# Products of a chunked recurrence on TensorE: both heads as one full-size product, and other regroupings

## The chip, the core and the metric

The kernel runs on one core of a Trainium2 chip. The metric is the device time of one execution in microseconds; lower is better. The engines are TensorE (PE in the profile: matrix products, with PEld for its weight loads), VectorE (DVE), ScalarE (ACT), GpSimd (POOL), and SyncE (SP), from whose queue all transfers are issued. Each engine works through its own queue in the order in which the program was written; semaphores tie the queues together.

## The reference

One step of a two-layer hybrid decoder for a prompt of 512 tokens and 8 sampled sequences of 8 tokens (576 columns in all), model width 1024, inner width 2048, 32 heads of 64. Layer 1 is RWKV-7 time mixing, layer 2 a causal pooling mixer. The part that matters is the recurrence of layer 1, per head a 64 by 64 state S:

```python
def wkv7_scan(S0, r, w, k, v, a, b):
    def step(S, inp):
        r_t, w_t, k_t, v_t, a_t, b_t = inp
        Sa = jnp.einsum('bhij,bhj->bhi', S, a_t)
        S = S * w_t[:, :, None, :] + Sa[..., None] * b_t[:, :, None, :] + v_t[..., None] * k_t[:, :, None, :]
        return S, jnp.einsum('bhij,bhj->bhi', S, r_t)
```

The inputs r, k, v and a gate z are projections of the normed input; the decay w and the rate a come from two low-rank paths. After the scan follow a group norm per head, a bonus term, the gate, and an output projection that is added to the residual stream. Then comes the pooling layer and a last norm.

## The kernel before

The recurrence is computed in chunks of 64 tokens: 8 chunks of the prompt, and the 64 sampled tokens as a ninth. Two heads make a pair (q = 0, 1) that fills the 128 partitions; 16 pairs (m). All products of the recurrence are in fp32, where one product is two instructions of TensorE; the projections are split into high and low parts and run as three reduced-precision products of 128 by 128 by 288 columns ("dense" here).

The work is a graph of operations. `Plan` holds them with nominal costs, and a list scheduler (`order`) writes out one fixed order for all engines from costs, from rotating buffers that must be free, and from a due time for each operation: the table `DUES`, by label (stage letter and number within the stage), plus a step per pair. Labels count on within a stage (`plan.n`), so an operation that disappears shifts the labels behind it unless the counter is moved by hand.

Three stretches follow one another. `front` computes k, v, the decay and what the recurrence needs, and spills it to DRAM (`a_d`, `bk_d`, `bkt_d`, `vt_d`, `p_d`). `rproj` makes r. Then the 16 pairs go through four steps, several pairs at a time:

- `prep(m)`: loads RA (a and r, rows of 576 columns) and BK (L964 to L978), makes the A products (L988: per chunk and head, 64 rows by 128 columns by 128 columns), masks them (L1001 to L1021), and inverts a triangular 32 by 32 block on GpSimd in 31 steps (L1049, L1055), through a round trip over DRAM; two small product groups (L1084, L1098) make the off-diagonal corner. The inverse stands in TI, 64 columns per chunk.
- `recur(m)`: the chain over the chunks. Each hop has three product steps, each one product per head with 64 output rows: the right-hand side (L1158, L1161), the solution with TI (L1180), and the state's change (L1198). Between them stand ScalarE copies out of PSUM (L1174, L1186) and VectorE's update of the state (L1211), which takes the decay at the chunk's end from Pc, loaded from `p_d` (L1116). The sampled sequences have products of their own (L1231, L1257), and the outputs two products per chunk and head (L1280, L1283), written chunk by chunk.
- `after(m)`: group norm, transposes back (L1376), gate, output projection (L1406, dense).
- `zgate(m)`: the gate's projection (L1428, dense).

PSUM in this stage: two banks "pa" for A products, corner, state update and transposes, two "ch" for the chain, one "yy" for outputs, one "sx" for the sampled sequences, two "oo" for the dense products. RA has 4 buffers, SV, UV and BKT 2 each, BK and the inverse's tiles one.

Of the kernel before, what the change touches and what calls it, by code (L numbers as in the profile page):

```python
# [26 lines left out]
# columns of the packed constants  # L27
# [7 lines left out]
# columns of the packed per-channel parameters  # L35
# [44 lines left out]
# where the scheduler's choices lie: a due time per operation of a stage ("-": as the code gives it), and per block a step  # L80
# [91 lines left out]
DXV, MK, ML, MV, MZ, MR = (0, 1), (0, 1, 2, 3), (), (0, 2, 4, 6), (), (0, 2, 4, 6)    # blocks whose mixing DVE does  # L172
NTI, NZ = 3, 2


class Later:
    """a tile that is allocated in the course of the plan"""
# [8 lines left out]
class Plan:  # L186
    """Operations with nominal costs (ns), and a list scheduler that puts them in order.  use: instances of rotating
    buffers, held from the first operation that uses one until the last has ended.  dense: projections, which run beside
    the small products of the recurrence at an even share, so that the tensor engine's clock stays up."""
    ENG = ["PE", "ACT", "DVE", "POOL", "SP", "NIL"]  # L190
    # from the end of one engine's operation to the start of another's that needs it; a transfer's issue
# [13 lines left out]
    def op(self, eng, dur, fn, need=(), use=(), due=0.0, dense=0, work=(0.0, 0.0)):  # L205
        """work: of a product's time the part that depends on the clock, and what it counts for the clock"""
# [8 lines left out]
    def order(self):  # L215
# [19 lines left out]
        taken = {b: [] for b in bufs}            # instances in the order in which they were taken  # L235
        held, done = {}, {}                      # instance: end of its users so far; released at
# [5 lines left out]
        while any(cand.values()):  # L242
            best = None
            for e in self.ENG:
                lo, pick = 1e17, []
                for i in cand[e]:
                    t = max(ready[i], free[e])
                    if ops[i][6] == 1 and share < 0:
                        t = max(t, free[e] - share / RATE)
                    for u in ops[i][4]:  # L250
                        if u not in held:
                            q, n = taken[u[0]], bufs[u[0]]
                            if len(q) >= n:
                                t = max(t, done.get(q[-n], 1e18))
# [59 lines left out]
def body(tc, nc, a):  # L314
# [18 lines left out]
    X1 = kp.tile([128, 16, T], F32R, name="X1")  # L333

# [35 lines left out]
    def split(src, hi, lo, hi_eng=None, lo_eng=None):  # L370
        """src = hi + lo, exact, both in the tensor engine's reduced float32"""
# [16 lines left out]
    def proj(ps, tag, ws, xs, nm, nk=8):  # L388
        """two bank tiles [128, HT] of  W^T x ; ws: list of (hi, lo) units of 8 k blocks"""
# [12 lines left out]
    def rsqrt(y, x, t, mul, eps):  # L402
        """y = (x mul + eps)^-1/2: Newton's iteration from the exponent's half, to float32's accuracy; x, t are used up"""
# [23 lines left out]
    def front(plan, bf, fps, fsb):  # L427
        """norm, token shift, k, v, decay and what goes into the recurrence"""
# [15 lines left out]
        # ---- norm  # L444
# [51 lines left out]
        # ---- mixes; order of mu: r, w, k, v, a, g  # L496
        lseq = []        # the low-rank mixes go in order
# [39 lines left out]
        # low-rank stage 1  # L537
# [21 lines left out]
        def pv(t):      # token columns as (chunk, 64) and (sequence, 8)  # L559
            return (t[:, :TP].rearrange("p (c j) -> p c j", j=64), t[:, TP:].rearrange("p (c j) -> p c j", j=8))  # L560
# [1091 lines left out]
```

## Time and profile before

| | us |
|---|---|
| median of 3 runs | 1626.28 |
| lowest, highest | 1624.1, 1642.92 |
| span of the profiled execution | 1632.8 |

| engine | busy us | share of the span |
|---|---|---|
| TensorE | 1487.4 | 91% |
| VectorE | 1020.8 | 63% |
| GpSimd | 729.6 | 45% |
| ScalarE | 638.4 | 39% |

The profile is of one execution. Its own time is given as the span from the first to the last instruction; what lies around the span isn't known apart from the median of the runs beside it. "Busy" counts instructions as the hardware recorded them. Ends of products are modelled and overlap, so distances between starts tell more of TensorE than durations do. The granted clock is the share of full speed that the throttle let through: 1.00 is 2.4 GHz, 0.50 is 1.2 GHz.

### The profile page before, as it was taken

Reading aid. Unit: us, or ns where it says so; the run is one execution under the profiler, and the core shown is the slowest. Engines: PE = TensorE matmul, PEld = TensorE weight load, DVE = VectorE, ACT = ScalarE, POOL = GpSimd, SP = SyncE. Lnnn points to the kernel's source line nnn. Section 1 sums busy time; section 2 is a strip of 40 time slices with the busy share of each in tenths; the row PEclk is TensorE's granted clock in tenths of the full one; section 3 lists DMA queues with packets and bytes.
Section 4 is the critical chain, followed back from the end, with each engine's and each line's share of the span. In section 5 each row is a group of like instructions: output and inputs, shape, how many; then the busy total and the mean of one; then the engine's idle time right before and its main releaser. Section 6 shows DMA issues by size and latency. Waiting matters only on the chain.

```text
span 1632.8 us, 33010 instructions
## 1 busy us (share of the span) xinstructions
PE 1487.4 (91%) x12544; PEld 1307.6 (80%) x12544; DVE 1020.8 (63%) x2007; ACT 638.4 (39%) x1663; POOL 729.6 (45%) x1374
## 2 busy tenths in 40 slices
PE   5678988987698999999999999999989999999996
PEld 4567888887687877777777777777767999999996
DVE  4688888889456443666666656566567574546223
ACT  3445544454332233444444434444434334234211
POOL 5956665658200533565656555556511240534000
PEclk8689998997898985899999989899899999999998
DMA  3026766564787774555555555554322332222221
GB/s 123 24 68 211 222 203 205 187 200 161 216 281 229 214 260 122 140 161 160 155 158 154 153 147 153 140 134 136 113 65 67 93 104 79 91 96 82 78 78 71
DMA packets 161359, 234.04 MB, mean 143 GB/s; under 512 B 76976, under 2 KB 94704, under 8 KB 161200
## 3 DMA queue, kind: packets, MB, share of 16 engines
q1 hardware_dynamic: 161200, 231.92, 47.2%
q8 instruction: 99, 1.62, 0.4%
q14 instruction: 60, 0.49, 0.1%
HBM read 162.30 MB, written 69.56 MB: 142 GB/s over the span
## 4 chain that ended last, share of the span: by engine, by line
PE 59%; DMA 8%; DVE 6%; issue 2%; SPq 1%; ACT 1%; POOL 1%; DVEq 0%; ACTq 0%; POOLq 0%
PE oo L1406 7%; PE ooz L1428 5%; PE oor L924 4%; PE paA L988 4%; PE ch L1198 2%; DMA SV<-vt_d 2%; PE u L384 2%; PE zz L384 2%; PE u L386 2%; PE u L385 2%; PE zz L386 2%; PE zz L385 2%; PE oo L386 2%; PE oo L384 2%; PE oo L385 2%
## 5 line engine op out<-in xcount | busy, mean ns | idle before, releaser
L1049 POOL TENSOR_TENSOR tm<-X,R 108x84 f32<-108x84 f32 (+23 forms) x465 | 146.7, 316 | 194.9 <-DMA TI<-xd 127.2
L1055 POOL TENSOR_TENSOR X<-X,tm 108x84 f32<-108x84 f32 (+23 forms) x465 | 150.2, 323 | 36.3 <-DMA TI<-xd 0.2
L372 ACT CAST wh_w<-wf_w 128x1024 fp32r<-128x1024 f32 x56 | 58.8, 1050 | 189.8 <-PE oo L385 74.0
L1412 DVE TENSOR_TENSOR late<-oo,late 128x288 f32<-128x288 f32 x256 | 109.3, 454 | 31.1 <-PE oo L1406 26.9
L530 PE MATMUL kvk<-X,wh_z 128*128 128x288 f32 x480 | 107.0, 316 | 16.6 <-ACT X L509 9.9
L1428 PE MATMUL ooz<-X,wh_z 128*128 128x288 f32 x448 | 117.1, 350 | 0.2
L373 DVE TENSOR_TENSOR wl_w<-wf_w,wh_w 128x1024 fp32r<-128x1024 f32 x56 | 79.9, 1427 | 46.5 <-ACT wh_w L372 46.5
L1211 DVE SCALAR_TENSOR_TENSOR SV<-SV,Pc,ch 64x64 f32<-64x64 f32 x192 | 53.8, 280 | 82.9 <-PE ch L1198 49.3
L530 PEld LDWEIGHTS kvk<-X,wh_z 128*128 128x128 f32 x480 | 83.1, 201 | 20.6 <-ACT X L509 10.5
L1428 PEld LDWEIGHTS ooz<-X,wh_z 128*128 128x128 f32 x448 | 74.3, 203 | 30.7 <-issue 21.2
L1406 PE MATMUL oo<-gh,wh_o 128*128 128x288 f32 x256 | 91.4, 357 | 2.8 <-DVE late L1412 2.7
L530 PE MATMUL kvv<-X3h,wl_o 128*128 128x288 f32 x256 | 82.4, 322 | 11.4 <-POOL wl_o L790 11.4
L530 PE MATMUL kvv<-X3h,wh_o 128*128 128x288 f32 x256 | 82.4, 322 | 9.4 <-ACT wh_o L786 8.8
L988 PE MATMUL paA<-RA,BK 64*128 64x128 f32 x576 | 86.5, 290 | 0.4 <-DMA BK<-bk_d 0.4
L786 ACT CAST wh_o<-wf 128x512 fp32r<-128x512 f32 (+1 forms) x84 | 49.6, 615 | 93.7 <-PE oo L1406 38.2
L1186 ACT COPY UV<-ch 64x64 f32<-64x64 f32 x256 | 53.2, 208 | 78.3 <-PE ch L1180 76.0
L530 PE MATMUL kvk<-X,wl_z 128*128 128x288 f32 x240 | 74.8, 312 | 7.6 <-POOL wl_z L790 7.5
L530 PE MATMUL kvv<-X3l,wh_o 128*128 128x288 f32 x256 | 80.9, 316 | 0.4 <-DVE X3l L513 0.4
L1406 PE MATMUL oo<-gl,wh_o 128*128 128x288 f32 x256 | 76.1, 297 | 1.0 <-DVE gl L1395 1.0
L1250 POOL TENSOR_TENSOR late<-late,Pc 128x512 f32<-128x512 f32 x16 | 17.0, 1060 | 134.0 <-PE sx L1231 134.0
L988 PEld LDWEIGHTS paA<-RA,BK 64*128 64x128 f32 x576 | 69.1, 187 | 9.0 <-ACT TI L1104 1.8
L384 PE MATMUL u<-XG,wh_w 128*128 128x288 f32 x256 | 75.5, 297 | 0.7 <-ACT wh_w L372 0.7
(303 smaller groups left out, 4901.9 us busy)
## 6 DMA issues: line engine op xcount, KB each, us to landing
wf_w<-in_w_in SPq DMA_DIRECT2D x32, 512.0 KB
bk_d<-BK SPq DMA_DIRECT2D x16, 576.0 KB
bkt_d<-BT SPq DMA_DIRECT2D x64, 144.0 KB
BK<-bk_d SPq DMA_DIRECT2D x16, 576.0 KB
BKT<-bkt_d SPq DMA_DIRECT2D x16, 576.0 KB
wf<-in_w_k SPq DMA_DIRECT2D x16, 512.0 KB
wf<-in_w_v SPq DMA_DIRECT2D x16, 512.0 KB
wf<-in_w_z SPq DMA_DIRECT2D x16, 512.0 KB
```

The source lines that it names most:

```text
L373: (lo_eng or V).tensor_tensor(out=lo, in0=src, in1=hi.bitcast(F32), op=ALU.subtract)
L384: PE.matmul(out, wh, xh, start=first, stop=False)
L385: PE.matmul(out, wh, xl, start=False, stop=False)
L386: PE.matmul(out, wl, xh, start=False, stop=last)
L530: PE.matmul(o, w_[:, k, :rows], hs(x_, h), start=k == 0 and i == 0, stop=k == KD - 1 and i == 2)
L924: PE.matmul(buf(*pk)[:, :HT], w_[:, k, :], hs(x_, h), start=k == 0 and i == 0, stop=k == KD - 1 and i == 2)
L988: PE.matmul(pt_[:, c - c0, :], buf("BK", m)[r0:r0 + 64, c, :], buf("RA", m)[r0:r0 + 64, q:q + 2, 64 * c:64 * c + 64], start=True, stop=True)
L1049: E.tensor_tensor(out=tm[:, :nq, :nt], in0=X[:, :nq, s:s + 1].broadcast_to([108, nq, nt]), in1=R[:, s:s + 1, s + 1:].broadcast_to([108, nq ...
L1055: E.tensor_tensor(out=X[:, :nq, s + 1:], in0=X[:, :nq, s + 1:], in1=tm[:, :nq, :nt], op=ALU.add)
L1406: PE.matmul(buf(*pk)[:, :HT], w_[:, mo, :], hs(x_, h), start=i == 0, stop=i == 2)
L1412: V.tensor_tensor(out=o, in0=buf(*pk)[:, :HT], in1=o, op=ALU.add)
L1428: PE.matmul(buf(*pk)[:, :HT], w_[:, k, :], hs(x_, h), start=k == 0 and i == 0, stop=k == KD - 1 and i == 2)
```

## The change

- The chain's three product steps become one product each for both heads: 128 rows, 128 output rows, 128 columns, with off-diagonal parts that are computed and not read. For that RA is laid out by chunk (9 chunks of 256 columns, r and a of the two heads beside one another), TI becomes block-diagonal with 128 columns a chunk and is cleared whole, and the unused state of chunk 0 is set to zero by GpSimd.
- The A products of both heads stand in one operation, alternating between heads, and take both "pa" banks. The planner counts two new instances of a buffer in one operation correctly.
- The products of the sampled states (four operations) become one, the two of the state update one.
- Outputs are made four chunks at a time: all products with the state first, then all with the solution.
- The transposes back take all 128 rows and half of the identity.
- The decays at the chunks' ends are kept on chip in `pcs`, written by GpSimd in `front`; the load of Pc in `recur` goes.
- The loads of RA write 64 columns at a place. The table of due times is the same, with the label counter moved so that labels keep their meaning. A scratch space is made smaller to free memory.

```diff
+    pcs = kp.tile([128, KC, 16], F32, name="pcs")
...
+            def f(m=m):
+                G.tensor_copy(pcs[:, m, 0:8].unsqueeze(2), pv(buf("Pc", m))[0][:, :, 63:64])
+                G.tensor_copy(pcs[:, m, 8:16].unsqueeze(2), pv(buf("Pc", m))[1][:, :, 7:8])
+            by["pcs", m] = op("POOL", 200, f, [ex[uPc]], [uPc], d0 + 13)
...
-            TIb.append(tail["lp"].tile([128, 9, 64], F32, name=f"TI{i}"))
+            TIb.append(tail["lp"].tile([128, 9, 128], F32, name=f"TI{i}"))
...
-    BUF = {"RA": ([128, 3, T], 4), "BK": ([128, 9, 128], 1), "Pc": ([128, T], 2), "UV": ([128, 4, 9, 32], 2),
+    BUF = {"RA": ([128, 9, 256], NRA), "BK": ([128, 9, 128], 1), "UV": ([128, 4, 9, 32], 2),
...
+    def ra(m, q, c):
+
+        return buf("RA", m)[64 * q:64 * q + 64, c].rearrange("p (s j) -> p s j", j=64)[:, 2 * q:2 * q + 2]
...
-            SP.dma_start(out=buf("RA", m)[:, 1, :], in_=r_d[m])
+            for r0, o in ((0, 0), (64, 192)):
+                SP.dma_start(out=buf("RA", m)[r0:r0 + 64, :, o:o + 64], in_=r_d[m][r0:r0 + 64].rearrange("p (c j) -> p c j", j=64))
...
+            pks = [("pa", "A", m, c0, q) for q in range(2)]
+
+            def f(c0=c0, n=n, pks=pks):
+                pts = [buf(*pk).rearrange("p (a b) -> p a b", b=128) for pk in pks]
+                for c in range(c0, c0 + n):
+                    for q in range(2):
+                        r0 = 64 * q
+                        PE.matmul(pts[q][:, c - c0, :], buf("BK", m)[r0:r0 + 64, c, :],
+                                  ra(m, q, c), start=True, stop=True)
...
-            V.transpose(buf("T1", m), TI[:, 0:8, 0:32])
+            for r0 in (0, 64):
+                V.transpose(buf("T1", m)[r0:r0 + 64], TI[r0:r0 + 64, 0:8, r0:r0 + 32])
...
-        def f():
-            SP.dma_start(out=buf("Pc", m), in_=p_d[m])
-        lPc = op("SP", 819, f, use=[uPc], due=due + 4)
+        lPc = by["pcs", m]
+        plan.n += 1
...
+        def f():
+            for q in range(2):
+                G.memset(buf("SV", m)[64 * q:64 * q + 64, 2 * q:2 * q + 2, 0, :], 0.0)
+        lSV.append(op("POOL", 240, f, use=[uSV], due=due))
...
-                for q in range(2):
-                    r0, k0 = 64 * q, 64 - 64 * q
-                    if c == 0:
-                        PE.matmul(rh[r0:r0 + 64], RA[k0:k0 + 64, 2 * q, 0:64], SV[k0:k0 + 64, 2 * q:2 * q + 2, c, :],
-                                  start=True, stop=True)
-                    else:
-                        PE.matmul(rh[r0:r0 + 64], RA[:, 2 * q, 64 * c:64 * c + 64], SV[:, 2 * q:2 * q + 2, c, :],
-                                  start=True, stop=True)
+                PE.matmul(tile()[:, lo:lo + 128], buf("RA", m)[:, c, 64:192], buf("SV", m)[:, :, c, :], start=True, stop=True)
...
-                for q in range(2):
-                    r0 = 64 * q
-                    PE.matmul(tile()[r0:r0 + 64, lo + 64:lo + 128], TI[r0:r0 + 64, c, :], buf(*rk)[r0:r0 + 64],
-                              start=True, stop=True)
+                PE.matmul(tile()[:, lo + 128:lo + 256], TI[:, c, :], buf(*rk), start=True, stop=True)
...
-                for q in range(2):
-                    PE.matmul(buf(*ck)[64 * q:64 * q + 64, 128:192], buf("BKT", m)[:, 64 * q:64 * q + 64, c],
-                              buf("UV", m)[:, 2 * q:2 * q + 2, c, :], start=True, stop=True)
+                PE.matmul(buf(*ck)[:, 256:384], buf("BKT", m)[:, :, c], buf("UV", m)[:, :, c, :], start=True, stop=True)
...
-                                               scalar=buf("Pc", m)[r0:r0 + 64, 64 * c + 63:64 * c + 64], in1=v2(dsp),
+                                               scalar=pcs[r0:r0 + 64, m, c:c + 1], in1=v2(dsp),
...
-        for c in range(9):
-            key, lo = (("yy", m), 64 * c) if c < 8 else (sk, 128)
...
+        for cs in ((0, 1, 2, 3), (4, 5, 6, 7), (8,)):
+            key, lo = (("yy", m), 0) if cs[0] < 8 else (sk, -128)
...
+                for c in cs:
+                    for q in range(2):
+                        r0, o = 64 * q, lo + 64 * c
+                        if c > 0:
+                            PE.matmul(t[r0:r0 + 64, o:o + 64], RA[r0:r0 + 64, c, 3 * r0:3 * r0 + 64],
+                                      SV[r0:r0 + 64, 2 * q:2 * q + 2, c, :], start=c in (1, 8), stop=False, skip_group_check=True)
+                for c in cs:
+                    for q in range(2):
+                        r0, o = 64 * q, lo + 64 * c
+                        PE.matmul(t[r0:r0 + 64, o:o + 64], W3[:, q, c, :], UV[:, 2 * q:2 * q + 2, c, :], start=False, stop=True,
+                                  skip_group_check=True)
...
-                        PE.matmul(buf(*pk)[r0:r0 + 64, 64 * (c - c0):64 * (c - c0) + 64], buf("yc", m)[r0:r0 + 64, c, :],
-                                  ident[r0:r0 + 64, r0:r0 + 64], start=True, stop=True)
+                        PE.matmul(buf(*pk)[r0:r0 + 64, 64 * (c - c0):64 * (c - c0) + 64], buf("yc", m)[:, c, :],
+                                  ident[:, r0:r0 + 64], start=True, stop=True)
```

## Rows read from the trace of the kernel before

**Rows 1.** The page's engine table: busy us, share of the span, instructions.

```profile
PE 1487.4 (91%) x12544; PEld 1307.6 (80%) x12544; DVE 1020.8 (63%) x2007; ACT 638.4 (39%) x1663; POOL 729.6 (45%) x1374
```

**Rows 2.** Windows: stretch, length, busy PE, PEld, DVE, ACT, POOL, granted clock, DMA share, GB/s.

```profile
600.00:700.00 100.00, 96.28 (x937) 72.16 (x934) 49.44 (x144) 41.28 (x157) 53.19 (x148) 0.71 0.54 159
800.00:900.00 100.00, 99.03 (x1141) 78.23 (x1139) 62.16 (x174) 46.24 (x168) 61.01 (x171) 1.00 0.56 155
...
620.00:640.00 20.00, 20.00 (x130) 15.23 (x128) 7.39 (x28) 4.07 (x17) 2.16 (x9) 0.50 0.62 152
```

**Rows 3.** Chain that ended last, 560 to 1250 us: start us, length us, what.

```profile
594.33 5.89 DMA wf<-in_w_o
...
774.09 1.08 PE paA L988 x8
...
931.98 1.08 PE paA L988 x8
```

**Rows 4.** Timeline, PE: start, us, line, operation, tiles, shape, count; 813.30 to 852.92.

```profile
813.30 1.16 PE L988 MATMUL paA<-RA,BK 64*128 64x128 f32 x8
...
815.15 0.29 PE L1406 MATMUL oo<-gh,wl_o 128*128 128x288 f32 x1
815.37 0.69 PE L1098 MATMUL pax<-TI,ZM 32*32 32x32 f32 x32
815.99 0.40 PE L1406 MATMUL oo<-gh,wh_o 128*128 128x288 f32 x1
816.23 0.30 PE L1406 MATMUL oo<-gl,wh_o 128*128 128x288 f32 x1
...
816.98 1.16 PE L988 MATMUL paA<-RA,BK 64*128 64x128 f32 x8
...
852.66 0.33 PE L1280 MATMUL yy<-SV,RA 64*64 64x64 f32 x4
852.92 0.34 PE L1283 MATMUL yy<-UV,W 128*64 128x64 f32 x4
```

**Rows 5.** Chain that ended last, 826 to 872 us: start us, length us, what.

```profile
843.32 0.58 PE pay L1376 x20
...
846.96 1.06 PE paS L1257 x2
```

**Rows 6.** Timeline, PE: A products of the ninth chunk, both heads, and one head.

```profile
519.70 0.49 PE L988 MATMUL paA<-RA,BK 64*128 64x128 f32 x4
...
826.31 0.49 PE L988 MATMUL paA<-RA,BK 64*128 64x128 f32 x2
```

**Rows 7.** Timeline, PE: fp32 products of full size among dense ones.

```profile
1552.30 0.30 PE L386 MATMUL oo<-X,wl_w 128*128 128x288 f32 x1
1552.43 1.13 PE L1486 MATMUL ssq<-sqb,cst 128*128 128x288 f32 x4
...
1553.53 0.30 PE L385 MATMUL oo<-X,wh_w 128*128 128x288 f32 x1
```

**Rows 8.** Groups by line, 560 to 1250 us: count, busy us, mean ns, idle before.

```profile
L1018 DVE TENSOR_TENSOR RA<-paA,cst 64x256 f32<-64x256 f32 (+1 forms) x82 | 29.4, 359 | 14.2 <-ACT AB L1001 12.0
...
L1001 ACT COPY AB<-paA 64x256 f32<-64x256 f32 x54 | 19.7, 365 | 46.1 <-PE paA L988 46.1
```

**Rows 9.** Timeline of GpSimd (one inverse and the next) and of SP's queue.

```profile
807.49 0.24 POOL L1049 TENSOR_TENSOR tm<-X,R 108x31 f32<-108x31 f32 x1 [0.30 <-DMA X<-in_cst]
...
831.36 0.23 POOL L1055 TENSOR_TENSOR X<-X,tm 108x11 f32<-108x11 f32 x1
...
847.73 0.24 POOL L1049 TENSOR_TENSOR tm<-X,R 108x31 f32<-108x31 f32 x1 [0.64 <-DMA TI<-xd]
...
876.48 2.92 SPq L1062 DMA_DIRECT2D xd<-X  x3
```

**Rows 10.** The page's DMA parts: packets by size; queue, packets, MB, share.

```profile
DMA packets 161359, 234.04 MB, mean 143 GB/s; under 512 B 76976, under 2 KB 94704, under 8 KB 161200
...
q1 hardware_dynamic: 161200, 231.92, 47.2%
```

More of the change, by code (lines that the diff above doesn't have):

```diff
@@ L173 @@
 NTI, NZ = 3, 2
+NRA = 4
 class Later:
@@ L249, in order @@
                         t = max(t, free[e] - share / RATE)
+                    new = {}
                     for u in ops[i][4]:
                         if u not in held:
-                            q, n = taken[u[0]], bufs[u[0]]
+                            q, n = taken[u[0]], bufs[u[0]] - new.get(u[0], 0)
+                            new[u[0]] = new.get(u[0], 0) + 1
                             if len(q) >= n:
@@ L835, in clear @@
         for i in range(NTI):
[L836 to L839 removed]
+            G.memset(TIb[i], 0.0)
     b3 = plan.op("POOL", 700 * NTI, clear, [b2], due=-1000)
@@ L890, in body @@
     PER = 30.0
-    by = {}
     rlast = []
@@ L1103, in f @@
             def f(r0=r0):
-                S.copy(out=TI[r0:r0 + 32, 0:8, 32:64], in_=buf(*px_)[r0:r0 + 32, 0:256].rearrange("p (c t) -> p c t", t=32))
+                S.copy(out=TI[r0:r0 + 32, 0:8, r0 + 32:r0 + 64], in_=buf(*px_)[r0:r0 + 32, 0:256].rearrange("p (c t) -> p c t", t=32))
             z4.append(op("ACT", 264, f, need=z3, use=[px_, ("TI", m)], due=due + 4))
@@ L1185, in f @@
                 def f(q=q):
-                    S.copy(out=buf("UV", m)[0:64, 2 * q:2 * q + 2, c, :], in_=v2(tile()[64 * q:64 * q + 64, lo + 64:lo + 128]))
+                    S.copy(out=buf("UV", m)[0:64, 2 * q:2 * q + 2, c, :], in_=v2(tile()[64 * q:64 * q + 64, lo + 128 + 64 * q:lo + 192 + 64 * q]))
                 es.append(op("ACT", 104, f, need=[mm, lUV], use=[key, uUV], due=due, dense=dn))
@@ L1222, in recur, with f @@
         sk = ("sx", m)
-        rst = []
-        for j in range(4):
-            def f(j=j):
-                RA, SS = buf("RA", m), buf("SS", m)
-                t = buf(*sk)[:, 0:128].rearrange("p (s t) -> p s t", s=2)
-                for b in (2 * j, 2 * j + 1):
-                    for q in range(2):
-                        r0 = 64 * q
-                        PE.matmul(t[r0:r0 + 64, :, 8 * b:8 * b + 8], SS[r0:r0 + 64, b, :],
-                                  RA[r0:r0 + 64, q:q + 2, TP + 8 * b:TP + 8 * b + 8], start=True, stop=True)
-            rst.append(op("PE", 330, f, need=[lSS] + by["A8", m], use=[uRA, uSS, sk], due=due + 3, work=(100, 57)))
+        def f():
+            SS = buf("SS", m)
+            t = buf(*sk)[:, 0:128].rearrange("p (s t) -> p s t", s=2)
+            for b in range(8):
+                for q in range(2):
+                    r0 = 64 * q
+                    PE.matmul(t[r0:r0 + 64, :, 8 * b:8 * b + 8], SS[r0:r0 + 64, b, :],
+                              ra(m, q, 8)[:, :, 8 * b:8 * b + 8], start=True, stop=True)
+        plan.n += 3
+        rst = [op("PE", 700, f, need=[lSS] + by["A8", m], use=[uRA, uSS, sk], due=due + 3, work=(400, 228))]
         rse = []
@@ L1236, in f @@
             def f(q=q):
-                S.copy(out=buf("RA", m)[64 * q:64 * q + 64, q:q + 2, TP:T],
+                S.copy(out=ra(m, q, 8),
                        in_=buf(*sk)[64 * q:64 * q + 64, 0:128].rearrange("p (s t) -> p s t", s=2))
             rse.append(op("ACT", 158, f, need=rst, use=[uRA, sk], due=due + 4))
-        UVe[8] = hop(8, "rhs8", sk, 0, rse + idn + by["A", m], due + 5)
+        UVe[8] = hop(8, "rhs8", sk, 128, rse + idn + by["A", m], due + 5)
         msk = []
@@ L1250, in f @@
             G.tensor_tensor(out=buf("SS", m), in0=buf("SS", m),
-                            in1=buf("Pc", m)[:, TP + 7:T:8].unsqueeze(2).broadcast_to([128, 8, 64]), op=ALU.mult)
-        ssm = op("POOL", 1001, f, need=rst + [lPc], use=[uSS, uPc], due=due + 8)
+                            in1=pcs[:, m, 8:16].unsqueeze(2).broadcast_to([128, 8, 64]), op=ALU.mult)
+        ssm = op("POOL", 1001, f, need=rst + [lPc], use=[uSS], due=due + 8)
         pk = ("pa", "S", m)
-        pm = []
-        for q in range(2):
-            def f(q=q):
+        def f():
+            for q in range(2):
                 PE.matmul(buf(*pk)[64 * q:64 * q + 64, :], buf("BKT", m)[:, 64 * q:64 * q + 64, 8],
                           buf("um", m)[:, q].rearrange("p b i -> p (b i)"), start=True, stop=True)
-            pm.append(op("PE", 460, f, need=msk[8 * q:8 * q + 8] + [lBKT], use=[uBKT, ("um", m), pk], due=due + 18, work=(450, 1444)))
+        plan.n += 1
+        pm = [op("PE", 1000, f, need=msk + [lBKT], use=[uBKT, ("um", m), pk], due=due + 18, work=(860, 2888))]
         def f():
@@ L1309, in f @@
         def f():
-            V.tensor_scalar(out=buf("yc", m)[:, 8], in0=buf(*sk)[:, 128:192], scalar1=sm(1)[:, 8:9], scalar2=None,
+            V.tensor_scalar(out=buf("yc", m)[:, 8], in0=buf(*sk)[:, 384:448], scalar1=sm(1)[:, 8:9], scalar2=None,
                             op0=ALU.subtract)
```

82 lines of the change are left out of this document (36 added, 46 removed), and 2 rows, old and new, of the table BUF.

## The prediction

> **What bounds the kernel now.** I read the page's engine table first, then the windows by stage, then the chain of work in order of time, then TensorE's timeline inside one period. TensorE is busy 91% of the span, the next engine 63% [rows 1]. The span falls into three stages: up to about 600 us the projections that prepare the recurrence, from 600 to 1240 us the recurrence over 16 head pairs, and then the pooling layer. All edits that matter lie in the middle one. There TensorE is busy 99.0 of 100 us at a granted clock of 1.00 (800 to 900 us), and even in the slow patch at 620 to 640 us it is busy 20.0 of 20 at 0.50, the 1.2 GHz level [rows 2]. So in this stage TensorE's queue is the limit, and what leaves that queue leaves the time.
>
> The A products of successive pairs stand on the chain at 774.09 and, four pairs on, at 931.98 [rows 3]: 157.89 / 4 = 39.5 us a pair.
>
> What fills the 39.5 us is to be seen in the timeline. The same two small products (four instructions) cost 0.26 us when the shape of the array changes in front of them (852.66 to 852.92) [rows 4]; twenty such instructions in one shape, five chunks, cost 0.58 us, 0.117 a chunk [rows 5]. So about 0.15 us of each 0.26 is the change of shape and the first weights after it. For an excursion from the dense projections: 815.15 to 815.37 is 0.22 where two dense starts in a row are 0.13 apart (1552.30 to 1552.43), and the return, 815.99 to 816.23, is 0.24 instead of 0.13 [rows 4, 7]. With 0.15 inside, an excursion costs 0.09 + 0.15 + 0.11 = 0.35 us. Counted over the period from 813.30 to 852.92 us [rows 4], the array changes shape 70 times: 36 times to or from the dense 128 by 128 shape (18 excursions) and 34 times between two smaller shapes. That is 18 x 0.35 + 34 x 0.15 = 11.4 us of the 39.5.
>
> **The change, part by part.**
>
> *Streaming time.* An fp32 product of full size with 288 columns: four instructions and one dense product take 1552.43 to 1553.53, so (1.10 - 0.13) / 4 = 0.243 an instruction [rows 7], 0.108 for 128 columns, 0.215 a product of two instructions. Chain: 26 steps a pair (three in each of eight chunks, two for the samples) go from 26 x 0.117 to 26 x 0.215, +2.55 us. The A products: 18 products, 18 x 0.215 = 3.87; with both heads side by side 1.94, so -1.93. That the halves do run side by side is shown once: four instructions, both heads, last 0.49 us, and two instructions of one head also 0.49 [rows 6]. The states' update (L1257): 1.06 us a head [rows 5], of which 512 columns are 2 x 0.43 = 0.86; both heads in one operation save 0.86 if column halves overlap like row halves, and nothing if not. Output products and transposes stream the same columns. Sum: 2.55 - 1.93 - 0.86 = -0.2 us, nothing. So the gain can't come from streaming.
>
> *Changes of shape.* Chain products now have the dense shape. Whether an fp32 product among reduced-precision ones costs a change all the same is answered by [rows 7]: it starts 0.13 us after the dense one before, and the whole sequence is filled by its streaming. So 26 chain steps cost no change next to dense work or to each other. What is left per pair: A 3 groups, sample states 1, state update 1, transposes 2, the two halves of the inverse's corner 2 + 2, outputs 3 groups with one inner change each: 14 excursions and 3 inner changes, 14 x 0.35 + 3 x 0.15 = 5.35 us, against 11.4. Gain 6.0 us a pair. Lower bound of the gain: if all 26 steps still paid 0.35, the gain is gone (11.4 - 5.35 - 9.1 = -3.0). Upper bound: if groups of one shape are placed side by side and only 8 excursions stay, 11.4 - 2.8 - 0.45 = 8.1. I take 6.0 + 0.2 = 6.2, since the fp32 row is the very operation, among the same neighbours.
>
> *Waits that come in.* An A operation now takes both banks of the "pa" ring, so it waits at the head of TensorE's queue until both are empty, and everything, dense work too, stands behind it. Emptying two banks costs two ScalarE copies of 0.365 and four VectorE operations of about 0.36, 2.2 us [rows 8]. Three such groups a pair: at worst 6.5 us a pair, at best nothing, since the written order puts other products between them (813.30 to 816.98 for two A groups today [rows 4]). I charge 0.5 us a pair. The chain's ScalarE copy becomes twice as wide, but with two chains in flight that is latency and not queue.
>
> *Off TensorE.* The decays' 16 loads of 288 KB go; their place is taken by small GpSimd copies in the first stage, where TensorE waits for other things. The RA loads are cut into 256-byte pieces, 2304 a pair instead of 256 longer ones. By the mean of all packets (47% of 16 engines' time over 161359 packets, 76 ns) [rows 10] this would be 2048 x 76 / 16 = 9.7 us of DMA time a pair; by bytes nothing. Half of today's packets are under 512 B already and carry few bytes, so I take 2 us, hidden: RA has four buffers and is loaded two pairs ahead. VectorE gets one more short transpose, GpSimd two small memsets a pair. The output products in groups of four start later, but only the last group is followed by anything. All this I cost at nothing; the cover is TensorE's own 33 us a pair.
>
> *Sum.* 39.5 - 6.2 + 0.5 = 33.8 us a pair; over 16 pairs 5.7 x 16 = 91 us. The clock: 600 to 700 us ran at 0.71 [rows 2], a loss of 29 us there; the stretch begins with a wait of 5.89 us for weights at 594 us [rows 3], and stays low although TensorE is busy. Full-size products are nearer to the dense work that runs at 1.00; I take a third of the loss back, 10 us (bounds: nothing, 29). Together 101 us: the profiled execution goes from 1632.8 us to 1532. That execution lies 0.4% above the median of the runs (1626.28), so the forecast is 1532 x 0.996 = **1526 us**.
>
> **The rivals.**
>
> *The inverse becomes the limit (chance 0.17).* GpSimd's 31 elimination steps run from 807.49 to 831.36, 24 us [rows 9], on single buffers. Before the next may begin, the result is written out (three issues, 2.92 us on SP's queue [rows 9]), and the buffer is loaded anew; today the gap is 831.36 to 847.73, 16 us, partly waiting for TensorE. A gap of 7 gives 31 us a pair, under 33.8; of 12, 36 us: then the gain is 3.5 x 16 = 56 us and the time 1632.8 - 56 = 1577, 1570 against the median. For it: GpSimd's queue also holds the group norm's work between inverses, in fixed order. Against it: its idle time today is mostly waiting for TensorE.
>
> *Only streaming counts (0.06).* If the change of shape is not saved, because the written order puts every chain step next to a smaller shape, the period stays at 39.5 - 0.2 and the time at 1623. The Trainium skill says something near this: "TensorE: Matmul & The Clock Gate", section "Part 3: Packing small matmuls — row/col tiling", advises against leaving the array part empty and reports up to 2.38 times the rate from packing three column tiles; undoing the packing of the chain would by that cost 26 x 0.1 x 16 = 41 us, and packing the A products return 31. No run here shows it for groups as short as these; in the trace short packed groups cost 0.26, not 0.117.
>
> *The clock gives it back (0.04, slower).* Place: the recurrence, after a wait of TensorE as at 594 us. At 620 to 640 us the granted clock is 0.50 with TensorE busy all the time [rows 2]. If new waits (both "pa" banks, the inverse) send each pair there, every 2 us at 1.2 GHz lose 1: with 12 us of each pair the gain of 5.7 is gone, with 16 us the time is 1632.8 + 2.3 x 16 = 1670, slower by over 2%. Against it: TensorE had hardly a gap at 800 to 900 us and ran at 1.00 there, with the smaller shapes of today.
>
> *More than forecast (0.10).* Groups lie together (8.1 instead of 6.0) and the whole loss of clock comes back: 1632.8 - 16 x 7.8 - 29 = 1479, so 1473.
>
> **How the numbers follow.** The forecast has 0.63, with its own range 1495 to 1555 (a wait of 0 to 2.3 us a pair and 0 to 20 us from the clock). The range that should hold the time eight times in ten reaches to the inverse's case and to part of the last: 1475 to 1585. A measurement of this kernel can tell about 2% from no change, so faster means under 1594: forecast, inverse (nearly all) and more-than-forecast, 0.63 + 0.16 + 0.10 = 0.89. Same: 0.06 + 0.01 = 0.07. Slower 0.04.
>
> **What would show it.** Right: L1198, L1161 and L1180 (under their new lines) as two instructions of about 0.11 us each starting 0.13 us after dense products; about 31 changes of shape a pair; A groups of 16 instructions in about 1.1 us; successive A groups of pairs 33 to 35 us apart with TensorE still over 93% busy; nothing saved before 450 and after 1240 us (old times). Wrong: TensorE idle in front of A groups with VectorE as releaser (banks); GpSimd without idle time and TensorE waiting for the inverse's corner (inverse); granted clocks under 0.8 in the middle of the recurrence (clock); chain products of 0.4 us or more (shape).

## The result and the profile after

The kernel after is slower: median 1711.61 us (1701.86 to 1715.34, four runs) against 1625.19 (1609.89 to 1642.92, four runs) before, a ratio of 1.0558 with the interval 1.0482 to 1.0634. Some executions of a kernel fall in a second, slower state, and the ratios leave them out (two of the four of e2 below), so that a ratio need not be that of the medians beside it. The forecast was 1526, range 1475 to 1585. The profiled execution has a span of 1713.3 us, 80.5 more than before.

The last stage is not touched. The last residual add of the recurrence on VectorE, first before, then after:

```profile
1242.45 0.46 DVE L1412 TENSOR_TENSOR late<-oo,late 128x288 f32<-128x288 f32 x1 [0.19 <-PE oo L1406]
```

```profile
1322.40 0.85 DVE L1426 TENSOR_TENSOR late<-oo,late 128x288 f32<-128x288 f32 x2 [0.37 <-PE oo L1420]
```

The recurrence ends at 1242.9 and at 1323.3 us, and what follows takes 390 us in both. All of the 80 us come from before that point, and the chain's third step says where: its products start from 594.2 to 1216.7 us before and from 599.3 to 1295.6 after, 622.5 and 696.3 us (source line of before under e5 below). So the recurrence itself is 74 us longer; 5 of the rest are its later start.

```profile
L1205 PEld LDWEIGHTS ch<-UV,BKT x256: 312/334/341, 599.3 to 1295.6; 128*128 128x128 f32 x128
```

After, the engine table (answers to [rows 1]):

```profile
PE 1479.9 (86%) x11712; PEld 1336.1 (78%) x11712; DVE 1020.6 (60%) x2023; ACT 644.9 (38%) x1663; POOL 750.3 (44%) x1429
```

The windows (answer to [rows 2]; stretch, length, busy PE, PEld, DVE, ACT, POOL, granted clock, DMA share, GB/s):

```profile
600.00:700.00 100.00, 86.98 (x743) 69.30 (x742) 53.53 (x156) 41.41 (x153) 49.73 (x139) 0.81 0.62 174
800.00:900.00 100.00, 88.76 (x888) 75.36 (x888) 55.76 (x159) 40.51 (x142) 58.11 (x163) 0.87 0.47 124
1000.00:1100.00 100.00, 91.12 (x803) 75.84 (x801) 55.42 (x158) 37.84 (x135) 54.48 (x152) 0.80 0.45 119
```

TensorE has 832 instructions fewer and is still busy for as long. In the middle of the recurrence it was busy 99% at a clock of 1.00; now it is 89% at 0.87. It has become an engine that waits, and it runs slower while it works. The same over one window, 600 to 1200 us, before and then after:

```profile
600.00:1200.00 600.00, 583.65 (x6276) 455.90 (x6273) 357.93 (x1033) 255.38 (x936) 330.22 (x929) 0.92 0.53 147
```

```profile
600.00:1200.00 600.00, 522.85 (x4842) 437.86 (x4840) 331.31 (x944) 232.80 (x831) 319.31 (x891) 0.84 0.51 132
```

Busy 583.65 and 522.85 of 600 us, clocks 0.92 and 0.84. Every other engine is less busy than before too, so none of them has become the limit. What TensorE waited for in these 600 us (us in total, times, longest), before and after:

```profile
PE ch L1158 <- DMA SV<-vt_d: 8.3, 5, 3.6
PE paz L1084 <- DVE T L1075: 2.8, 4, 0.8
PE ch L1198 <- ACT UV L1186: 2.0, 4, 0.6
```

```profile
PE paz L1099 <- DVE T L1090: 22.0, 10, 4.2
PE oo L1420 <- DVE late L1426: 17.7, 34, 3.2
PE ch L1172 <- DMA SV<-vt_d: 6.5, 4, 2.8
PE ch L1172 <- DVE SV L1217: 4.8, 10, 0.8
...
PE paA L999 <- DVE late L1395: 0.6, 1, 0.6
```

These are many waits of different kinds: for the inverse's transpose, for the residual add that empties the "oo" banks, for the state. The one that the forecast charged, an A group that waits for its two banks, is the last line: 0.6 us. One place, on the chain in order of time after:

```profile
853.66 6.19 DMA o_wkvs<-late
859.87 2.57 DMA late<-in_swkv
862.48 1.11 PE sx L1236 x32
863.59 0.99 PE oo L1420 x6
```

A store has to leave a buffer, the next state is loaded into it, and only then come the samples' products, which stand at the head of TensorE's queue with dense work behind them. The places of the old chain that [rows 3, 5] show are TensorE's own products but for one transfer. Over the whole span the chain was PE to 59% before and is to 47% now, with DMA 11% and VectorE 10%.

What the products cost can be read where TensorE does not wait (start us, us, line, shape, count; answers to [rows 4]):

```profile
627.59 0.62 PE L1205 MATMUL ch<-UV,BKT 128*128 128x128 f32 x2
628.05 0.39 PE L1172 MATMUL ch<-SV,RA 128*128 128x128 f32 x2
628.19 0.52 PE L1442 MATMUL ooz<-X,wh_z 128*128 128x288 f32 x2
628.54 0.29 PE L1442 MATMUL ooz<-X,wl_z 128*128 128x288 f32 x1
628.67 0.43 PE L1442 MATMUL ooz<-X,wh_z 128*128 128x288 f32 x2
628.94 0.30 PE L1442 MATMUL ooz<-X,wl_z 128*128 128x288 f32 x1
...
629.29 0.39 PE L1189 MATMUL ch<-rhs,TI 128*128 128x128 f32 x2
629.44 0.51 PE L1442 MATMUL ooz<-X,wh_z 128*128 128x288 f32 x2
629.78 0.30 PE L1442 MATMUL ooz<-X,wl_z 128*128 128x288 f32 x1
...
632.64 1.16 PE L999 MATMUL paA<-RA,BK 64*128 64x128 f32 x16
633.74 0.49 PE L1172 MATMUL ch<-SV,RA 128*128 128x128 f32 x2
```

From the start of one of the chain's first two steps to the next start it is 0.14 and 0.15 us. That is not yet their whole cost: the two dense products behind such a step take 628.54 - 628.19 = 0.35 us, where two others take 628.94 - 628.67 = 0.27. With these 0.08 us a step costs 0.22, as forecast (0.215). The A group of 16 instructions costs 1.10, as forecast too. The third step costs 628.05 - 627.59 = 0.46, twice the forecast.

### The profile page after: what moved, and what is told of

Its sections match the earlier page's. It is cut to its first block, busy times and chain, and to the rows that moved or that the text cites. A ratio compares the mean times of both kernels' runs of the same rounds, so it can differ in the third digit from the quotient of the medians.

```text
span 1713.3 us, 31396 instructions
## 1 busy us (share of the span) xinstructions
PE 1479.9 (86%) x11712; PEld 1336.1 (78%) x11712; DVE 1020.6 (60%) x2023; ACT 644.9 (38%) x1663; POOL 750.3 (44%) x1429
## 2 busy tenths in 40 slices
DMA packets 192073, 229.20 MB, mean 134 GB/s; under 512 B 113841, under 2 KB 131569, under 8 KB 191921
## 3 DMA queue, kind: packets, MB, share of 16 engines
q1 hardware_dynamic: 191920, 227.20, 45.8%
## 4 chain that ended last, share of the span: by engine, by line
PE 47%; DMA 11%; DVE 10%; POOL 5%; issue 3%; SPq 3%; ACT 3%; DVEq 0%; POOLq 0%; ACTq 0%
PE ooz L1442 4%; PE ch L1205 4%; PE oo L1420 3%; PE ch L1189 2%; DMA xd<-X 2%; PE ch L1172 2%; PE u L388 2%; PE zz L388 2%; PE zz L390 2%; PE u L390 2%; PE u L389 2%; PE zz L389 2%; PE oo L390 2%; PE oo L388 2%; PE oo L389 2%
## 5 line engine op out<-in xcount | busy, mean ns | idle before, releaser
L1063 POOL TENSOR_TENSOR tm<-X,R 108x84 f32<-108x84 f32 (+23 forms) x465 | 154.7, 333 | 233.6 <-DMA TI<-xd 160.2
L1069 POOL TENSOR_TENSOR X<-X,tm 108x84 f32<-108x84 f32 (+23 forms) x465 | 155.1, 334 | 34.8
L1420 PE MATMUL oo<-gh,wh_o 128*128 128x288 f32 x256 | 100.4, 392 | 27.1 <-DVE late L1426 20.2
L1442 PE MATMUL ooz<-X,wh_z 128*128 128x288 f32 x448 | 113.2, 340 | 0.5 <-DVE late L1426 0.5
L1420 PEld LDWEIGHTS oo<-gh,wh_o 128*128 128x128 f32 x256 | 53.8, 210 | 58.1 <-DVE late L1426 39.5
L1217 DVE SCALAR_TENSOR_TENSOR SV<-SV,pcs,ch 64x64 f32<-64x64 f32 x192 | 53.7, 279 | 72.8 <-PE ch L1205 69.3
L1205 PE MATMUL ch<-UV,BKT 128*128 128x128 f32 x256 | 89.6, 435 | 3.9 <-ACT UV L1194 2.9
L1420 PE MATMUL oo<-gl,wh_o 128*128 128x288 f32 x256 | 83.5, 326 | 2.7 <-DVE gl L1409 2.6
L1420 PE MATMUL oo<-gh,wl_o 128*128 128x288 f32 x256 | 82.2, 321 | 0.5 <-DVE wl_o L799 0.5
L1205 PEld LDWEIGHTS ch<-UV,BKT 128*128 128x128 f32 x256 | 70.7, 325 | 13.6 <-ACT UV L1194 7.7
```

The source lines that it names most:

```text
L1063: E.tensor_tensor(out=tm[:, :nq, :nt], in0=X[:, :nq, s:s + 1].broadcast_to([108, nq, nt]), in1=R[:, s:s + 1, s + 1:].broadcast_to([108, nq ...
L1069: E.tensor_tensor(out=X[:, :nq, s + 1:], in0=X[:, :nq, s + 1:], in1=tm[:, :nq, :nt], op=ALU.add)
L1205: PE.matmul(buf(*ck)[:, 256:384], buf("BKT", m)[:, :, c], buf("UV", m)[:, :, c, :], start=True, stop=True)
L1420: PE.matmul(buf(*pk)[:, :HT], w_[:, mo, :], hs(x_, h), start=i == 0, stop=i == 2)
L1442: PE.matmul(buf(*pk)[:, :HT], w_[:, k, :], hs(x_, h), start=k == 0 and i == 0, stop=k == KD - 1 and i == 2)
```

## The experiments

The first question was whether the order or the products had made the loss. The planner writes one order from costs, buffers and the table of due times. The change alters costs, buffers and operations, and takes the old table over.

### One nominal cost, by one nanosecond (e1)

```diff
-            mm = op("PE", 165, hop_rhs(c, tile, lo, need, due), need=need, ...
+            mm = op("PE", 166, hop_rhs(c, tile, lo, need, due), need=need, ...
```

This is the kernel before with the same instructions on every engine; only the order that the planner works out differs.

> The kernel before with one nominal cost of the planner changed by 1 ns (the chain's first product step, 165 to 166); no instruction is changed, only the order in which they are written out. Theory O (the loss of the change comes from the written order: the due times were found for the old graph and its costs, and any other costs give another, worse order): slower than before by 20 to 80 us, with TensorE's idle time up and its granted clock down in the stretch 600 to 1300 us. Theory P (the loss comes from the full-size products themselves: L1205 takes 0.45 to 0.63 us where 0.22 was forecast, and longer steps of the chain): within 10 us of before. Theory W (new waits from the change: both pa banks in one operation, the loads of RA in small pieces): within 10 us of before.

1661.04 us, ratio 1.0235 (1.0164 to 1.0306); the 13 runs of the kernel before beside it lie between 1611.49 and 1659.07. A nanosecond in the planner's books costs 2.4% of the time. One half of the expectation did not come, though: TensorE's idle time is not up. Its window:

```profile
600.00:1200.00 600.00, 583.29 (x6074) 452.05 (x6072) 348.99 (x999) 245.24 (x902) 325.18 (x918) 0.89 0.50 140
```

Busy 583.29 us as before (583.65), at a clock of 0.89 instead of 0.92. What e1 lost in the recurrence, it lost to the clock and not to waits.

### The new costs without the new products (e2)

```diff
-            mm = op("PE", 165, hop_rhs(...), ..., work=(110, 267 if dn else 100), dense=dn)
+            mm = op("PE", 224, hop_rhs(...), ..., work=(213, 512), dense=dn)
...
-            e = op("ACT", 104, f, need=[mm], use=[key, rk], due=due, dense=dn)
+            e = op("ACT", 157, f, need=[mm], use=[key, rk], due=due, dense=dn)
```

The other two steps of a hop take the same costs. Again no instruction of the kernel before is changed.

> The kernel before with the changed kernel's nominal costs of the chain steps (165 to 224 for the three products, 104 to 157 for the copy, with their clock counts); again no instruction is changed, only the written order. O: slower by 40 to 120 us, like the changed kernel. P and W: within 10 us of before.

1756.33 us, ratio 1.0728 (1.0617 to 1.0838). The new costs alone, put into the old graph with the old table, lose at least as much as the whole change does. So the table fitted neither of the two neighbours of its graph that were tried.

### The new products without the new order (e3)

```diff
+                PE.matmul(tile()[:, lo:lo + 128], RA[:, c, 64:192], SV[:, :, c, :], start=True, stop=True)
...
+                PE.matmul(tile()[:, lo + 128:lo + 256], TI[:, c, :], buf(*rk), start=True, stop=True)
...
+                PE.matmul(buf(*ck)[:, 256:384], buf("BKT", m)[:, :, c], buf("UV", m)[:, :, c, :], start=True, stop=True)
```

The chain's three steps are of full size, with the layouts of RA and TI and the decays on chip, inside the operations and the order of the kernel before. A products, outputs and the rest stay as they were.

> The kernel before with the chain's products of full size (and RA and TI laid out for that, the decays kept on chip, the unused state of chunk 0 cleared by VectorE), written out in exactly the order of before; A products, sample states, outputs and transposes as before. By the sequence of before, 50 instead of 70 changes of shape a pair remain. O: the products are worth what their prices say: 20 x 0.15 saved, 2.55 of streaming added, and 8 x 0.25 us added if the third step costs 0.47 as in the changed kernel: about 1.5 us a pair more, so 0 to 30 us slower than before, TensorE without idle time and the granted clock as before. P: slower by 50 to 90 us. W (loads of RA in small pieces): slower, with TensorE or the chain waiting for RA.

1633.56 us, ratio 1.0064 (1.0015 to 1.0113). The windows:

```profile
600.00:800.00 200.00, 193.59 (x1716) 158.04 (x1714) 118.38 (x356) 86.29 (x312) 111.37 (x316) 0.93 0.56 146
800.00:1000.00 200.00, 198.32 (x1912) 165.41 (x1909) 129.91 (x372) 89.32 (x316) 116.04 (x335) 1.00 0.57 145
1000.00:1200.00 200.00, 196.79 (x1920) 162.83 (x1920) 125.78 (x364) 89.17 (x318) 99.79 (x274) 1.00 0.48 125
```

TensorE is as busy as before and at a clock of 1.00 from 800 us on (the expectation had left the clock as it was), yet nothing is gained. Two A groups that are three pairs apart:

```profile
814.69 1.16 PE L993 MATMUL paA<-RA,BK 64*128 64x128 f32 x8
936.61 1.16 PE L993 MATMUL paA<-RA,BK 64*128 64x128 f32 x8
```

That is 40.6 us a pair; before, it was 39.5 [rows 3], at a clock of 1.00 as well. So the full-size chain costs 1.1 us a pair in TensorE's own time (1.5 were expected), and the higher clock in the rest of the stretch pays it back. It can't be the cause of the 5.6%, but it isn't the gain of the forecast either.

### The same graph, due times made for it (e4)

```diff
-            if o[8] in DUE:
-                due[i] = DUE[o[8]] + STEP[o[8][0]] * o[9]
+            due[i] = float(RANK[i])
```

This is the kernel after, every instruction of it, with a rank for each operation in place of the due times. The ranks come from a search for a short plan by the kernel's own nominal costs.

> The changed kernel, all instructions the same, but with due times found anew for its own graph and nominal costs, operation by operation, with the same list scheduler (the due times of before were not made for it). O: most of the loss goes: 1560 to 1640 us, TensorE over 93% busy and the granted clock over 0.93 in the recurrence. P and W: within 25 us of the changed kernel's 1711.

1596.63 us, ratio 0.9837 (0.9771 to 0.9903): by the two ratios 7% faster than the kernel after, with the same instructions. The chain's third step runs from 582.5 us, 17 earlier than after, and takes 589.7 us instead of 696.3:

```profile
L1359 PEld LDWEIGHTS ch<-UV,BKT x256: 312/334/339, 582.5 to 1172.2; 128*128 128x128 f32 x128
```

The waits of the 600 us, the first lines:

```profile
PE paz L1253 <- DVE T L1244: 8.5, 13, 2.0
PE pay L1544 <- POOL late L1524: 6.1, 5, 2.9
PE ch L1326 <- DMA SV<-vt_d: 5.5, 7, 1.9
```

TensorE is busy 545.65 of 600 us there, 91% and not the 93% that were expected, at a clock of 0.95. The wait for the inverse went from 22.0 to 8.5 us without the inverse being any shorter, and the one for the residual add from 17.7 to 4.1.

### The third step's weights (e5, e6)

The full-size third step reads its weights as `BKT[:, :, c]`, 128 columns that lie nine elements apart. The weight loads of its source line, before (L1198), in e3 (L1195) and in e5 (L1195); count, shortest / median / longest in ns, first and last start, shapes:

```profile
L1198 PEld LDWEIGHTS ch<-UV,BKT x512: 193/217/227, 594.2 to 1216.7; 128*64 128x64 f32 x171
```

```profile
L1195 PEld LDWEIGHTS ch<-UV,BKT x256: 312/334/341, 592.1 to 1212.9; 128*128 128x128 f32 x128
```

```profile
L1195 PEld LDWEIGHTS ch<-UV,BKT x256: 186/189/338, 597.6 to 1187.3; 128*128 128x128 f32 x128
```

The edit of both experiments, on e3 and on e4. The columns that it reads hold other elements of the tile, so e5 and e6 give the time of such a read and leave out the recurrence's right result:

```diff
-                PE.matmul(..., buf("BKT", m)[:, :, c], buf("UV", m)[:, :, c, :], ...)
+                PE.matmul(..., buf("BKT", m).rearrange("p i c -> p (i c)")[:, 128 * c:128 * c + 128], buf("UV", m)[:, :, c, :], ...)
```

> e3_chain_only once more (the order of before, chain products full size), and the third chain step (L1195) reads its weights as 128 neighbouring columns of BKT instead of 128 columns nine elements apart. The columns so read hold other elements of the same tile, so this kernel multiplies by wrong factors; what it measures is the time of the read alone. Theory S (the stride is the price that the forecast left out of the third step): weight loads of this line fall from 0.334 to about 0.206 us, two for each product, 8 products a pair, so -2.0 us for each of the 16 pairs while PE is the bound: about 1600 us against the 1633.6 of e3, and the period from 40.6 to about 38.6 us. Theory P (a full-size product is dear at this place whatever its weights): loads stay near 0.33 us, period 40.6 us, 1634 us.

1609.38 us against 1627.9, ratio 0.989 (0.9818 to 0.9961), where e3 had 1.0064. Again two A groups three pairs apart:

```profile
807.30 0.93 PE L993 MATMUL paA<-RA,BK 64*128 64x128 f32 x6
924.08 1.16 PE L993 MATMUL paA<-RA,BK 64*128 64x128 f32 x8
```

A load takes 189 instead of 334 ns, the period is 38.9 us instead of 40.6, and 16 x 1.7 = 27 us is what the runs show (24 by the medians, 28 by the ratios). The stride was the dear part of the full-size chain. Without it the chain costs 0.6 us a pair less than the two half products of the kernel before.

> e4_new_order once more (the kernel after with due times made for it), with the third chain step's weights read from 128 neighbouring columns, as in e5 and with the same wrong factors. Theory S: 16 pairs x 2.0 us = 33 us less where PE is the bound; PE stood idle 9% in this stretch of e4, so between 20 and 33 us: 1564 to 1577 us against 1596.6. Theory W (what is left above the forecast is waits of DVE, POOL and the transfers around the inverse, which the shorter products do not move): less than 8 us of gain, 1589 us or more.

1589.15 us, ratio 0.9759 (0.9691 to 0.9827): 7 us less than e4 by the medians and 13 by the ratios, whose intervals overlap; not 20 to 33. The loads are short here as well (189 ns), but TensorE is busy 536.82 of the 600 us instead of 545.65, at a clock of 0.93 instead of 0.95. Part of what the products gave back turned into waiting, and part went to the clock. In an order with 9% of waits the shorter product was worth at most half of what it was worth in the tight order of e5.

### A whole version, twice (e7, e8)

To use the packed read with the right factors, BKT has to be laid out anew:

```diff
-            SP.dma_start(out=buf("BKT", m), in_=bkt_d[m]...)
+            SP.dma_start(out=buf("BKs", m, 0), in_=bkt_d[m]...[:, 0:2])
...
+                S.copy(out=buf("BKT", m).rearrange("p c (a i) -> p a c i", a=4)[:, 2 * h:2 * h + 2], in_=buf("BKs", m, h))
...
-                PE.matmul(buf(*ck)[:, 256:384], buf("BKT", m)[:, :, c], buf("UV", m)[:, :, c, :], start=True, stop=True)
+                PE.matmul(buf(*ck)[:, 256:384], buf("BKT", m)[:, c, :], buf("UV", m)[:, :, c, :], start=True, stop=True)
```

e7 and e8 are this one kernel with two orders. For e7 the search used durations read from e6's trace:

> The kernel after, complete again, with two edits. (1) The third chain step's weights are packed: BKT is loaded in two halves in another layout and a ScalarE copy of 128x576 for each half (a 576-column copy is about 0.78 us in the rows) lays them out in runs of 128 columns; the DVE transposes that make BT write runs of 32 instead of every ninth element. (2) The order is worked out with durations read from e6's trace: a transfer lands 2.6 to 6.4 us after its issue (medians by kind there) where the written-out durations allowed about 1.6 to 3.1, SyncE issues one in 0.42 us, the groups of small products take what they took in e6. Theory W (what e4 and e6 left above the forecast is waits behind transfers and DVE that the old durations did not foresee, so another order of the same work takes them away): PE idle in 600 to 1200 us falls from 10.5% (e6) to under 5%, 1589 less 35 to 80 us: 1510 to 1555 us. Theory B (the waits belong to the chain of one pair, inverse, transfers and chain steps, and no order hides them): idle stays at 9 to 11% and the copies cost a little: 1580 to 1600 us.

1636.0 us, ratio 1.008 (1.0034 to 1.0127). Neither theory held: TensorE's idle time stayed at 10.6%, as theory B had it, but the time rose by 47 us over e6. The first waits:

```profile
PE ch L1343 <- DVE SV L1388: 13.8, 25, 1.9
PE ch L1376 <- ACT UV L1365: 7.1, 15, 1.0
PE ch L1360 <- ACT rhs L1356: 5.3, 12, 0.9
```

They are now inside the chain: a product stands at the head of the queue and its operand is a little late. From the start of a chain step to TensorE's next work it is 0.453 us in the mean of all 384 steps, 0.342 in e6.

For e8 the search used the kernel's own nominal costs again (and, which the expectation does not say, a small weight on the trace's durations):

> The same complete kernel as e7 (packed weights for the third chain step), with the order worked out by the durations that the kernel's own operations are written with, as in e4, not by those read from e6's trace. e7 showed a mean of 0.453 us from a chain product to PE's next work, e6 0.344, at equal idle of PE: an order timed to the trace leaves no slack between a chain product and the ScalarE copy that the next one needs. Theory M (that missing slack is what e7 lost): the chain returns to about 0.35 us, 382 x 0.10 = 39 us less than e7, and the packed weights keep what they gave e6: 1580 to 1600 us. Theory C (the ScalarE copies and the second load of BKT are what e7 lost): they stand here too, so 1620 to 1640 us.

1578.4 us, ratio 0.9725 (0.9664 to 0.9785). The copies and the second load stand in it too, so theory C is out, and the distance is back at 0.339 us, as theory M had it (the time is just under M's range). That the missing slack is what e7 lost is not shown, however. The third step's loads in e7 and in e8:

```profile
L1376 PEld LDWEIGHTS ch<-UV,BKT x256: 186/189/338, 606.0 to 1216.2; 128*128 128x128 f32 x128
```

```profile
L1376 PEld LDWEIGHTS ch<-UV,BKT x256: 186/189/338, 582.9 to 1158.1; 128*128 128x128 f32 x128
```

Of the 58 us between the two, 23 are lost before the chain begins. The chain itself is 35 us longer, and by the windows 30 of these are TensorE's busy time, at a clock of 0.89 instead of 0.92, and 5 its idle time: the waits inside the chain came in place of others. This version is complete and faster than both kernels. Its window:

```profile
600.00:1200.00 600.00, 537.98 (x5835) 457.57 (x5834) 396.59 (x1145) 295.59 (x998) 324.42 (x915) 0.92 0.52 139
```

## Why the prediction was wrong

A sum over the recurrence shows which terms held. The length is that of the chain's third step from first to last start, divided by 16 pairs; the busy share and the clock are means over 600 to 1200 us. The last three columns, in us a pair, are worked out from these.

| | length us | busy share | clock | a pair | idle | busy | busy x clock |
|---|---|---|---|---|---|---|---|
| before | 622.5 | 0.973 | 0.92 | 38.9 | 1.1 | 37.9 | 34.9 |
| e1, same instructions as before | 648.6 | 0.972 | 0.89 | 40.5 | 1.1 | 39.4 | 35.1 |
| after | 696.3 | 0.871 | 0.84 | 43.5 | 5.6 | 37.9 | 31.8 |
| e4, same instructions as after | 589.7 | 0.909 | 0.95 | 36.9 | 3.4 | 33.5 | 31.8 |
| e6, as e4 with packed weights | 582.3 | 0.895 | 0.93 | 36.4 | 3.8 | 32.6 | 30.3 |
| e8, packed weights, copies, another order | 575.2 | 0.897 | 0.92 | 36.0 | 3.7 | 32.2 | 29.7 |

The last column is an estimate of TensorE's work as it would last at the full clock. It comes out the same in the two orders of the kernel after, and nearly so in before and e1. Part of the first and the last pairs' work lies outside this stretch, so its rows are to be compared with one another and not with the 39.5 us of a pair. Nor are its differences exact: e3 and e5 come to 37.3 and 35.4 by it, 2.4 and 0.5 above before, where their periods say 1.1 above and 0.6 below.

So a pair takes 4.6 us more after than before: about 3 less by TensorE's work, 4.5 more by its idle time, and about 3 more by the clock.

**TensorE's own time: right in kind, about half in size.** 6.2 us a pair were to leave its queue; by the table some 3.1 left it (34.9 to 31.8), and 4.6 to 5.2 with packed weights. The chain's first two steps (0.22) and the A groups (1.10) cost what they should.

**The third step: mis-sized.** "0.215 a product of two instructions" was taken from a row whose weights lie side by side [rows 7] and put on all 26 steps. For 8 of them a pair the weights lie nine elements apart, and the step costs 0.46. That is the sign set for the rival of the shape (0.4 us or more), but e5 shows that the stride is the reason: 1.7 us a pair, 27 us of the time. In the table it is the step from 31.8 to 30.3. The trace of before had the sign of it, in a row that the forecast did not use: loads of 64 strided columns at 217 ns, more than 128 packed ones take (189 in e5).

**The waits: the step that failed.** "At best nothing, since the written order puts other products between them", and 0.5 us a pair was charged. But that written order is of the old graph. The change took the table over and altered the costs, the banks and the operations that the planner puts in order by it. e1 shows that 1 ns in one of these costs is worth 2.4%, e2 that the chain's new costs alone are worth 7%, e4 that the same instructions in an order made for them gain 7%. In place of the 0.5 stand 5.6 us a pair idle. Before, from 657 us on, the A groups of a pair stand at nearly the same distances in one pair after another; after, they are 4 to 27 us apart with no pattern. They are irregular in e4 too (4 to 15 us), so irregular distances alone are not the fault; which of the many waits came first is not shown. The wait that the forecast named (the "pa" banks) cost 0.6 us of the 600. Of the signs that were to show the forecast right, the shape of the products and of the A groups came, and a period of 33 to 35 us with TensorE over 93% busy did not.

**The clock: wrong sign.** A third of the loss of 29 us was to come back; the clock fell from 0.92 to 0.84. From e4 to the kernel after the busy time a pair rises from 33.5 to 37.9 us, the same work at the lower clock. So of the 6.6 us a pair between these two, 2.2 are idle time and 4.4 the clock. That is the rival "the clock gives it back" in its sign and its place, at a chance of 0.04 (its own sign, clocks under 0.8, was just missed: 0.80 to 0.87). Its mechanism, that new waits send TensorE to the lower level, is not shown: e1 idles no more than before and runs at 0.89 instead of 0.92. What sets the clock in one order and another stays open. The full-size products did go with the higher clock in the order of before: 1.00 from 800 us on in e3.

**The rivals.** *The inverse becomes the limit*: TensorE does wait for it (22.0 us), but GpSimd itself stood idle in front of the inverse's first operation, 233.6 us over the whole span where it was 194.9 before; in 600 to 1200 us 89 and 17. e4 takes TensorE's wait down to 8.5 with the inverse as long as ever. It was late, not too long.

```profile
L1063 POOL TENSOR_TENSOR tm<-X,R 108x84 f32<-108x84 f32 (+23 forms) x465 | 154.7, 333 | 233.6 <-DMA TI<-xd 160.2 <-DMA R<-rd 28.2 <-DMA X<-in_cst 8.8
```

*Only streaming counts*: out, since the first two steps of the chain cost 0.22 us beside dense work, their streaming alone. The Trainium skill, "TensorE: Matmul & The Clock Gate", section "Part 3: Packing small matmuls — row/col tiling", which was named there, would have the chain stay packed. e5 measured it: with packed weights, the unpacked chain is 0.6 us a pair shorter, not longer, so for these groups of two half products the advice does not hold; with strided weights (e3) it is 1.1 longer.

**Costed at nothing, and rightly.** RA's short pieces: packets rose to 192073, of which 113841 are under 512 B, and the queue's share of the 16 engines is 45.8% instead of 47.2 [rows 10]. The last stage is as long as before.

**Costed at nothing, and wrongly in this order.** The two small memsets that GpSimd got for each pair. In 600 to 1200 us its queue, which holds the inverse too, stood 60 us in front of them, mostly until products and updates were done with the state's buffer; the largest line after, and the same in e4:

```profile
POOL SV L1149 <- PE yy L1288: 26.9, 4, 10.4
```

```profile
POOL SV L1303 <- PE yy L1442: 6.4, 5, 3.1
```

e4 has the same memsets, so this is the order again; what it cost TensorE is not known apart.

**What stays open.** e8 idles 3.7 us a pair, and its clock is 0.92; without the idle time alone it would take about 1578 - 16 x 3.7 = 1519 us, an estimate, near the forecast. Whether an order exists that has neither, or whether the inverse, its transfers and the chain of one pair set a floor at about 36 us, these runs do not settle: the two orders of e7 and e8 differ by 58 us and neither is known to be the best. Nor was the kernel before run with a table searched anew, so how much of e4's gain over before comes from the search alone isn't known.

## What to carry to other kernels

An order written from costs and due times is part of the tuning, like a tile size. When a change touches an operation's cost, its buffers or its number, cost the change on the assumption that the old order is gone, and make the order anew before the change is judged. The saving of TensorE's own time was there and the kernel was slower all the same, because the old order did not carry over: what kept TensorE at 99% was that order, too, and not the work alone. When a cost is taken from a row, look whether the operand lies as it does in that row.

## What the runs showed of the hardware

- A weight load of fp32 with 128 columns took 189 ns with the columns side by side and 334 ns nine elements apart; 64 columns nine elements apart took 217 ns (source lines above).
- In the same order and at nearly the same busy share (97 and 98%), a chain of full-size products instead of two half ones went with a granted clock over 600 to 1200 us of 0.98 instead of 0.92 (e3 and before).
- The same instructions in another order, at the same busy share (97%), ran at a clock of 0.89 instead of 0.92 over this stretch (e1 and before).
- Two orders of the same instructions, 10.6 and 10.3% idle, ran at clocks of 0.89 and 0.92 over this stretch (e7, e8). Many waits of under 1 us inside the chain went with the lower one.
- The copies that lay BKT out anew (two ScalarE copies of 128x576 a pair, 671 ns each in the mean) and a second load did not keep e8 from being the fastest run; what they cost is not known apart.
